# Moving a data-dependent branch behind a pair of expert products in a two-layer mixture-of-experts kernel

## The chip, the core and the metric

The kernel runs on one core of a Trainium2 chip, in one launch. The metric is the device time of that launch in microseconds. Before the change the median of three runs is 868.0 us (867.71 to 869.29); the execution that was profiled took 868.12 us.

The engines are called by their profile names: PE (matrix products; PEld is its weight load), DVE (the vector engine), ACT (the scalar engine), POOL (GpSimd), SP (the queue that issues the weight DMAs). Each engine runs its own list of instructions in order. A compiler step reorders the instructions of the kernel's text within the limits of their dependences and writes each engine's list down; a branch stands in the list of every engine that has an instruction in it.

## The reference, cut to what matters

Two transformer layers over 256 tokens of width 1024, in fp32. Each ends with a mixture of 16 experts, top 2 of one group of 4, which is what the change touches:

```python
def grouped_moe(h, router_w, router_bias, w_gate, w_up, w_down):
    ...
    combine = jnp.sum(jax.nn.one_hot(idx, N_EXPERTS, dtype=jnp.float32) * w[..., None], axis=1).astype(h.dtype)
    y = jnp.zeros_like(hf)
    for e in range(N_EXPERTS):
        a = jax.nn.silu(hf @ w_gate[e]) * (hf @ w_up[e])
        y = y + combine[:, e:e + 1] * (a @ w_down[e])
    return y.reshape(B, S, D)
```

Ahead of the experts of each layer stands an attention (forgetting attention in the first layer, latent attention in the second); between the layers the keys and values of the second are made.

## The kernel before, in words

`moe(l, ...)` is called once for each layer (l = 0, 1). A one-hot matrix `P` gathers up to `CAP = 64` tokens for each expert, so that the experts are worked in pairs, two of 64 rows, i = 0 to 7. For each pair the loop at the end of `moe` does:

- `wide("g", i, 4)`: the gate products, 16 matrix products into PSUM bank 4 (L899; each fp32 product shows as two records, so 32 records);
- ACT's silu of bank 4 (L984), while `wide("u", i, 5)` makes the up products in bank 5 (L899, 32 records);
- DVE's product of both (L995), the transposes (L1002), their copy `aT` (L1005, L1006);
- the down products in banks 6 and 7, in two halves p = 0, 1 (L1017, 16 records each), DVE's gate multiply `yb` (L1030) and the two parts `yh` (ACT L1032, DVE L1033);
- `scatter(i - 1)`: 8 products (L911) that add the pair before to the four accumulator banks 0 to 3. In the text it stands behind the up products of pair i.

After an odd pair, `fetch` gathers the tokens of the next four experts: products L869 into banks 5 and 4, copied out by ACT (L877) and DVE (L875); `slots(i + 1, 5)` makes the next pair's scatter matrix in bank 5 (L883, DVE L886 and L889).

Weights come in 1 MB units, four for the gate, four for the up and four for the down products of each pair, on SP's queue in the order of their use. `get` looks a unit up, `done` gives its place back, and only then SP issues a later unit (L250 into a ring, L262 into pieces of other tiles that have come free). They come to some 100 MB for a layer.

An expert may draw more than 64 tokens. `overflow()` covers that: each engine loads the largest count (L916) and takes the branch `tc.If(vmax > CAP)` (L917). Its body, which uses banks 5, 6 and 7, `yb`, the tiles of tag "t2" and the accumulators, is long and is not entered with these inputs: no instruction of it is in the trace. At the other end of the branch every engine raises its semaphores by what the body would have added, and goes on. An instruction behind the branch that shares a tile with the body waits for those raised counts; one that shares nothing doesn't. In the text the branch stands ahead of the gate products of pair `OV = 4`, the fifth. A hint to PE (`mark_branch_hint_location`, "LikelyTaken") names the target of the branch; it is queued behind the last down product of half p = 0 of the fourth pair.

Of the kernel before, what the change touches and what calls it, by code (L numbers as in the profile page):

```python
# [43 lines left out]
OV = 4  # L44
# [29 lines left out]
def trunk_kernel(ctx, tc, A, out):  # L74
# [10 lines left out]
    def bank(i):  # L85
        return psp.tile([128, 512], F32, name=f"b{i}", tag=f"b{i}")
# [11 lines left out]
    def wide_rows(nm, l, i):  # L98
        return ((0, 4), (4, 2), (6, 2)) if l and nm == "u" and i == E // 2 - 1 else ((0, 4), (4, 4))
# [165 lines left out]
    def give(l, *names):  # L265
        for tags in SPARE[l]:
            if tags[-1] in names:
                spare.append((l, tags))
        issue()

    def get(name):
        assert name in live, name
        return live[name]
# [11 lines left out]
    def done(name):  # L285
        assert stream[state["used"]][0] == name, (stream[state["used"]][0], name)
        drop()
        mods()
# [239 lines left out]
    def squares(t, half, junk=None, src=None):  # L528
        cs = slice(512 * half, 512 * half + 512)
        if junk is None:  # L530
            junk = big.tile([128, 512], F32, name="junk", tag="yb", bufs=2)
        SC.activation(junk, x[:, t, cs] if src is None else src, AF.Square, accum_out=ssq[:, t, half:half + 1])
# [214 lines left out]
    def moe(l, G, sh, acc):  # L747
# [112 lines left out]
        def fetch(g, c, b):  # L860

            if c % 2 == 0:
                XG[g, c // 2] = big.tile([128, 4, 256], F32, name="XG", tag="qa", bufs=2)
            dst = XG[g, c // 2]
            ps = bank(b)
            for kk in range(2):
                k = 2 * c + kk
                for n in range(4):
                    at = PE.matmul(ps[:, 256 * kk:256 * kk + 256], xs[n % 2, n // 2][:, 128 * k:128 * k + 128],  # L869
                                   P[g][:, n // 2].rearrange("p e s -> p (e s)"), start=n == 0, stop=n == 3)  # L870
            for kk in range(2):
                k = 2 * c + kk
                src = ps[:, 256 * kk:256 * kk + 256]
                if kk:
                    V.tensor_scalar(dst[:, k % 4, :], src, G[:, k:k + 1], sh[:, k:k + 1], op0=ALU.mult, op1=ALU.add)  # L875
                else:
                    SC.activation(dst[:, k % 4, :], src, AF.Identity, scale=G[:, k:k + 1], bias=sh[:, k:k + 1])  # L877
            return at.ins
# [12 lines left out]
        def wide(nm, i, b):  # L891
            ps = bank(b)
            for c, (k0, nk) in enumerate(wide_rows(nm, l, i)):
                ws = [get((nm, l, i, c, e)) for e in range(2)]
                for kk in range(nk):
                    k = k0 + kk
                    for e in range(2):
                        o = 128 * (i % 2) + 64 * e
                        last = PE.matmul(ps[64 * e:64 * e + 64, :], XG[i // 2, k // 4][:, k % 4, o:o + 64], ws[e][:, kk, :],  # L899
                                         start=k == 0, stop=k == 7).ins  # L900
                if i == 0 and nm == "g":
                    after[5] = last
                for e in range(2):
                    done((nm, l, i, c, e))
            return ps

        def scatter(i):
            for half in range(2):
                for t in range(T):
                    for j in range(2):  # L910
                        PE.matmul(acc[t, half], PT[i][:, t, :], yh[:, j, 512 * half:512 * half + 512],  # L911
                                  start=False, stop=False)
# [61 lines left out]
            SC.activation(bank_, x[:, t, 512 * half:512 * half + 512], AF.Copy)  # L974
        give(l, "x")
        for i in range(E // 2):
            if i == OV:
                overflow()
            pg = wide("g", i, 4)
            if l and i == 0 and G2IN:  # L980
                with behind(5):
                    fin_bc("g2_1", "g2")
# [10 lines left out]
            pu = wide("u", i, 5)  # L993
            a = wk.tile([128, F], F32, name="act", tag="t2", bufs=3)
            V.scalar_tensor_tensor(a, sg, cs[:, i:i + 1], pu, op0=ALU.mult, op1=ALU.mult)  # L995
            if i:
                scatter(i - 1)
            if l and i == 2:
                final_gain()
# [11 lines left out]
            for p, (c0, n) in enumerate(cols):  # L1011
                py = bank(6 + p % 2)
                cs_ = slice(c0, c0 + n)
                ws = [get(("d", l, i, p, e)) for e in range(2)]
                for k in range(4):
                    for e in range(2):
                        at = PE.matmul(py[64 * e:64 * e + 64, 0:n], aT[:, k, 64 * e:64 * e + 64], ws[e][:, k, :],  # L1017
                                       start=k == 0, stop=k == 3).ins
                if i == OV - 1 and p == 0:
                    with tc.issue_after(at):  # L1020
                        tc.mark_branch_hint_location(f"over{l}", "LikelyTaken", [mybir.EngineType.PE])
                for e in range(2):
                    done(("d", l, i, p, e))
                if p == 0 and turn_over:
                    for c in range(2, 4):
                        fetch(i // 2 + 1, c, (5, 4)[c % 2])
                if p == 0 and i < E // 2 - 1:
                    slots(i + 1, 5)
                yb = big.tile([128, 512], F32, name="yb", bufs=2)
                V.tensor_tensor(yb[:, 0:n], py[:, 0:n], M[f"g2_{l}"][:, cs_], op=ALU.mult)  # L1030
                if len(cols) == 2 or p == 0:
                    SC.activation(yh[:, 0, cs_], yb, AF.Copy)  # L1032
                    V.tensor_tensor(yh[:, 1, cs_], yb, yh[:, 0, cs_].bitcast(F32), op=ALU.subtract)  # L1033
                    parts_ = [(PT[i], yh[:, j, cs_]) for j in range(2)]
                else:
                    parts_ = [(PT[i].bitcast(F32), yb[:, 0:n])]
                if i == E // 2 - 1:
                    half, o = c0 // 512, c0 % 512
                    if l == 0 and p == 0:
                        x.new()  # L1040
                    for t in range(T):
                        for j, (pt, y_) in enumerate(parts_):
                            PE.matmul(acc[t, half][:, o:o + n], pt[:, t, :], y_, start=False,
                                      stop=o + n == 512 and j == len(parts_) - 1)
                        if o + n == 512:
                            ch = slice(512 * half, 512 * half + 512)
                            if l == 0:
                                V.tensor_copy(x[:, t, ch], acc[t, half])
                            squares(t, half, None, acc[t, half])
                    if l and o + n == 512:  # L1050
                        gains(half, acc)
# [337 lines left out]
```

## Time and profile before

| what | value |
|---|---|
| median of three runs | 868.0 us (867.71 to 869.29) |
| profiled execution | 868.12 us, of which the span from first to last instruction is 866.1 us |
| PE busy | 776.4 us, 90% of the span |
| DVE, ACT, POOL busy | 375.4, 266.3, 163.0 us |
| mean granted TensorE clock | 0.962 of full speed |
| read from HBM | 294.30 MB, 341 GB/s over the span |

The page of the profile gives busy times of the engines, the span in 40 slices (with the granted clock and the share of the DMA engines) and the costliest groups of instructions. The trace behind it tells each instruction's start, its time and, where an engine sat idle, what ended the wait. In a timeline a row is: start in us, duration in us, engine, line, operation, tiles, count of the merged instructions and, in brackets, the idle time ahead with the releaser. An engine name with a q (PEldq, DVEq) stands for its sequencer, which waits, branches and issues.

### The profile page before, as it was taken

The numbers are of one execution on the slowest core, as the hardware profiler recorded it, in microseconds if no ns is written. First come the engines' busy times: TensorE is split into PE (matmuls) and PEld (weight loads), VectorE is DVE, ScalarE is ACT, GpSimd is POOL, SyncE is SP. The second block draws the span as 40 slices with busy tenths as digits, with TensorE's granted clock in tenths as the row PEclk, the third lists the DMA queues.
The fourth block names the chain that finished last, engine by engine and source line by source line (L and its number), as shares of the span: only waits on it lengthen the run. The fifth ranks groups of instructions, "written<-read, shape, count | busy, mean of one in ns | idle before, by whom it ended". The sixth has DMA issues, their size and how long they took to land.

```text
span 866.1 us, 11932 instructions
## 1 busy us (share of the span) xinstructions
PE 776.4 (90%) x4522; PEld 447.1 (52%) x4522; DVE 375.4 (43%) x831; ACT 266.3 (31%) x578; POOL 163.0 (19%) x151
## 2 busy tenths in 40 slices
PE   5688999998999999999978998999799997999995
PEld 3477888665344343243336766876434343334332
DVE  2488599967122222131159867665412223022112
ACT  1346455543111010010045745866211111001002
POOL 1364477320000000000019653221000000000000
PEclk9599999999999999999989998999799999899998
DMA  9997797899999999999995969668599999999671
GB/s 346 384 375 278 264 347 278 306 390 392 418 394 393 415 409 402 410 414 405 404 403 184 303 222 406 230 231 297 186 398 391 416 403 398 400 401 391 260 274 66
DMA packets 102854, 296.31 MB, mean 342 GB/s; under 512 B 6992, under 2 KB 26624, under 8 KB 90496
## 3 DMA queue, kind: packets, MB, share of 16 engines
q1 hardware_dynamic: 101968, 293.79, 89.9%
q10 hardware_dynamic: 288, 1.05, 0.3%
q8 instruction: 38, 0.62, 0.3%
q0 software_dynamic: 528, 0.59, 0.2%
q14 instruction: 32, 0.26, 0.1%
HBM read 294.30 MB, written 1.05 MB: 341 GB/s over the span
## 4 chain that ended last, share of the span: by engine, by line
issue 29%; PE 24%; DVE 5%; DMA 2%; ACT 1%; POOLq 0%; POOL 0%; another core or an unknown queue 0%; ACTq 0%; DVEq 0%
PE b L899 7%; PE b L1017 4%; PE b L522 2%; PE b L523 2%; PE b L524 2%; DVE macc L329 1%; PE b L911 1%; DMA fg<-in_final_norm_g_dram 1%; DVE wl L518 1%; PE b L631 1%; DMA w<-in_w_mod_dram 1%; DMA w<-in_exp_w_gate_dram 1%; PE b L321 1%; PE b L593 1%; PE b L557 1%
## 5 line engine op out<-in xcount | busy, mean ns | idle before, releaser
L899 PE MATMUL b<-w,XG 128*64 128x512 f32 x1024 | 241.9, 596 | 6.5 <-DVEq L917 6.1
L518 POOL TENSOR_TENSOR wl<-w,wh 128x512 fp32r<-128x512 f32 (+3 forms) x90 | 129.3, 1450 | 357.0 <-ACT wh L517 349.7
L899 PEld LDWEIGHTS b<-w,XG 128*64 128x64 f32 x1024 | 77.5, 137 | 148.2 <-issue 142.1
L1017 PE MATMUL b<-w,aT 128*64 128x512 f32 (+1 forms) x528 | 125.6, 585 | 3.7 <-ACT aT L1005 3.7
L995 DVE SCALAR_TENSOR_TENSOR act<-sg,rcs,b 128x512 f32<-128x512 f32 x16 | 12.0, 747 | 222.9 <-PE b L899 222.9
L517 ACT ACTIVATE wh<-w 128x512 fp32r<-128x512 f32 (+3 forms) x136 | 76.6, 587 | 66.0 <-PE b L524 27.4
L1017 PEld LDWEIGHTS b<-w,aT 128*64 128x64 f32 x528 | 38.3, 136 | 66.4 <-issue 56.7
L329 DVE SCALAR_TENSOR_TENSOR macc<-w,cact,macc 128x1024 f32<-128x1024 f32 x42 | 63.7, 1517 | 2.5 <-DMA w<-in_w_mod_dram 2.0
L1032 ACT ACTIVATE yh<-yb 128x512 fp32r<-128x512 f32 x31 | 19.5, 630 | 116.6 <-DVE yb L1030 109.5
L518 DVE TENSOR_TENSOR wl<-w,wh 128x512 fp32r<-128x512 f32 (+2 forms) x46 | 44.2, 970 | 20.2 <-ACT wh L517 20.0
L1030 DVE TENSOR_TENSOR yb<-b,g 128x512 f32<-128x512 f32 (+1 forms) x33 | 22.2, 674 | 67.5 <-PE b L1017 67.5
L984 ACT ACTIVATE sg<-b 128x512 f32<-128x512 f32 x16 | 9.6, 597 | 134.1 <-PE b L899 134.1
L539 POOL TENSOR_TENSOR rs<-rs,mhalf 128x1 f32<-128x1 f32 (+1 forms) x9 | 5.4, 600 | 218.2 <-DVE rs L538 218.2
L524 PE MATMUL b<-h,wl 128*128 128x256 f32 (+1 forms) x136 | 41.1, 304 | 3.5 <-DVE wl L518 3.4
L522 PE MATMUL b<-h,wh 128*128 128x256 f32 (+1 forms) x136 | 41.0, 304 | 3.4 <-ACT h L579 3.4
L321 PE MATMUL b<-w,cact 128*32 128x256 f32 x512 | 39.8, 419 | 4.7 <-DMA w<-in_w_mod_dram 4.4
L869 PEld LDWEIGHTS b<-P,xs 128*128 128x128 f32 x256 | 34.4, 203 | 14.4 <-issue 6.9
L1005 ACT ACTIVATE aT<-b 128x256 f32<-128x256 f32 x16 | 6.1, 384 | 114.1 <-PE b L1002 114.1
L869 PE MATMUL b<-P,xs 128*128 128x256 f32 x256 | 39.1, 304 | 1.6 <-DVE P L834 1.6
L523 PE MATMUL b<-h,wh 128*128 128x256 f32 (+1 forms) x136 | 40.2, 296 | 0.0
L911 PE MATMUL b<-yh,PT 128*128 128x512 f32 x112 | 36.0, 438 | 2.7 <-ACT yh L1032 2.1
L911 PEld LDWEIGHTS b<-yh,PT 128*128 128x128 f32 x112 | 19.6, 197 | 28.2 <-issue 17.0
(296 smaller groups left out, 1230.0 us busy)
## 6 DMA issues: line engine op xcount, KB each, us to landing
w<-in_exp_w_down_dram SPq DMA_DIRECT2D x50, 1024.0 KB, 12.4
w<-in_w_mod_dram SPq DMA_DIRECT2D x48, 1024.0 KB, 9.0
w<-in_exp_w_gate_dram SPq DMA_DIRECT2D x48, 1024.0 KB, 12.4
w<-in_exp_w_up_dram SPq DMA_DIRECT2D x48, 1024.0 KB, 13.2
w<-in_a_w_in_dram SPq DMA_DIRECT2D x12, 1024.0 KB, 12.3
w<-in_exp_w_gate_dram SPq DMA_DIRECT2D x42, 256.0 KB, 7.1
w<-in_exp_w_up_dram SPq DMA_DIRECT2D x40, 256.0 KB, 6.6
w<-in_kv_w_mod_dram SPq DMA_DIRECT2D x8, 1024.0 KB, 7.4
```

Of the source, the lines that this page charges most:

```text
L321: PE.matmul(acc[32 * q:32 * q + 32, :], cact[:, k:k + 1].to_broadcast([128, 32]), w[:, kk, 256 * q:256 * q + 256], start=k == 0, stop=k == 7)
L329: V.scalar_tensor_tensor(acc, w[:, kk, :], cact[:, k:k + 1], acc, op0=ALU.mult, op1=ALU.add)
L517: SC.activation(hi, src, AF.Copy)
L518: lo_eng.tensor_tensor(lo, src, hi.bitcast(F32), op=ALU.subtract)
L522: PE.matmul(ps, l[0], r_[0], start=start, stop=False)
L523: PE.matmul(ps, l[0], r_[1], start=False, stop=False)
L524: PE.matmul(ps, l[1], r_[0], start=False, stop=stop)
L869: at = PE.matmul(ps[:, 256 * kk:256 * kk + 256], xs[n % 2, n // 2][:, 128 * k:128 * k + 128], P[g][:, n // 2].rearrange("p e s -> p (e s)" ...
L899: last = PE.matmul(ps[64 * e:64 * e + 64, :], XG[i // 2, k // 4][:, k % 4, o:o + 64], ws[e][:, kk, :], start=k == 0, stop=k == 7).ins
L911: PE.matmul(acc[t, half], PT[i][:, t, :], yh[:, j, 512 * half:512 * half + 512], start=False, stop=False)
L1017: at = PE.matmul(py[64 * e:64 * e + 64, 0:n], aT[:, k, 64 * e:64 * e + 64], ws[e][:, k, :], start=k == 0, stop=k == 3).ins
L1030: V.tensor_tensor(yb[:, 0:n], py[:, 0:n], M[f"g2_{l}"][:, cs_], op=ALU.mult)
```

## The change

In the text of the pair loop the gate products of every pair now stand first; at the fifth pair `scatter(3)` follows them, then the branch. `scatter` is left out at its old place for that pair. The hint for PE moves from half p = 0 to half p = 1 of the fourth pair's down products.

```diff
         for i in range(E // 2):
+            pg = wide("g", i, 4)
             if i == OV:
+                scatter(i - 1)
                 overflow()
-            pg = wide("g", i, 4)
...
-            if i:
+            if i and i != OV:
                 scatter(i - 1)
...
-                if i == OV - 1 and p == 0:
+                if i == OV - 1 and p == 1:
                     with tc.issue_after(at):
                         tc.mark_branch_hint_location(f"over{l}", "LikelyTaken", [mybir.EngineType.PE])
```

## Rows read from the trace of the kernel before

**Rows 1.** Page: busy us, share of the span, instructions.
```profile
PE 776.4 (90%) x4522; PEld 447.1 (52%) x4522; DVE 375.4 (43%) x831; ACT 266.3 (31%) x578; POOL 163.0 (19%) x151
```

**Rows 2.** PE's waits: waiter, releaser, total us, times, longest us.
```profile
PE b L899 <- DVEq L917: 6.1, 1, 6.1
```

**Rows 3.** Timeline of PE, second layer, about the branch.
```profile
728.38 1.22 PE L869 MATMUL b<-P,xs 128*128 128x256 f32 x8
729.44 0.35 PE L883 MATMUL b<-idc,P 128*128 128x160 f32 x2
730.09 0.46 PE L911 MATMUL b<-yh,PT 128*128 128x512 f32 x1 [0.30 <-PEq L917]
736.65 1.94 PE L899 MATMUL b<-w,XG 128*64 128x512 f32 x2 [6.10 <-DVEq L917]
738.52 3.35 PE L911 MATMUL b<-yh,PT 128*128 128x512 f32 x7
741.81 13.98 PE L899 MATMUL b<-w,XG 128*64 128x512 f32 x62
```

**Rows 4.** The branch's own line, second layer: durations in ns, first and last start.
```profile
L917 PEldq EVENT_SEMAPHORE  x2: 51/51/51, 729.8 to 730.0; - x2
...
L917 DVEq EVENT_SEMAPHORE  x2: 21/21/21, 736.5 to 736.6; - x2
L917 PEldq COMPARE_BRANCH  x1: 439/439/439, 728.6 to 728.6; - x1
...
L917 DVEq COMPARE_BRANCH  x1: 68/68/68, 730.8 to 730.8; - x1
L917 SPq COMPARE_BRANCH  x1: 53/53/53, 743.2 to 743.2; - x1
```

**Rows 5.** Timelines of DVE and of ACT, second layer, about the branch.
```profile
731.25 0.54 DVE L875 TENSOR_SCALAR XG<-b,c_sc,c_sh 128x256 f32<-128x256 f32 x1
...
752.45 0.60 ACT L984 ACTIVATE sg<-b 128x512 f32<-128x512 f32 x1 [22.05 <-PE b L899]
```

**Rows 6.** The branch's own line, first layer.
```profile
L917 DVEq EVENT_SEMAPHORE  x2: 21/21/21, 332.6 to 332.7; - x2
L917 PEldq COMPARE_BRANCH  x1: 482/482/482, 322.9 to 322.9; - x1
...
L917 DVEq COMPARE_BRANCH  x1: 72/72/72, 326.9 to 326.9; - x1
```

**Rows 7.** Timeline of PE, first layer, about the branch.
```profile
324.63 0.45 PE L883 MATMUL b<-idc,P 128*128 128x160 f32 x2
325.01 1.07 PE L899 MATMUL b<-w,XG 128*64 128x512 f32 x2
326.38 2.10 PE L911 MATMUL b<-yh,PT 128*128 128x512 f32 x8 [0.30 <-PEq L917]
328.42 13.95 PE L899 MATMUL b<-w,XG 128*64 128x512 f32 x62
```

**Rows 8.** Stretches: us, busy PE, PEld, DVE, ACT, POOL (count), granted clock, DMA share, GB/s.
```profile
735.10:741.90 6.80, 5.25 (x11) 2.54 (x13) 0.00 (x0) 0.00 (x0) 0.00 (x0) 0.50 1.05 385
...
801.00:866.00 65.00, 52.17 (x242) 19.97 (x240) 12.38 (x26) 7.77 (x17) 0.72 (x1) 0.96 0.55 201
```

**Rows 9.** Timeline of PE, second layer, the third pair, without a branch.
```profile
675.07 1.22 PE L869 MATMUL b<-P,xs 128*128 128x256 f32 x8
...
678.33 13.95 PE L899 MATMUL b<-w,XG 128*64 128x512 f32 x64
```

**Rows 10.** PE's waits, all of the stretch 742 to 866 us.
```profile
PE b L1002 <- DVE act L995: 3.7, 4, 0.9
PE b L1043 <- DVE yb L1030: 1.7, 1, 1.7
PE b L1017 <- ACT aT L1005: 1.2, 3, 0.5
```

**Rows 11.** The hint's instruction on PE's sequencer (it is on line 1385).
```profile
L1385 PEldq BRANCH_PREFETCH_HINT  x2: 41/43/45, 314.8 to 722.4; - x2
```

## The prediction

> **What bounds the kernel now.** I read the page first: PE is busy for 776.4 us of the 866.1 [rows 1], so the question is where PE stands still. The list of PE's waits names the branch: in one place PE waited 6.1 us for DVE at line 917 [rows 2]. The timeline of PE shows the place, the fifth pair of the second layer: after the slot products (L883) one scatter record at 730.09, then nothing until 736.65; two product records and seven scatter records then take 1.94 and 3.35 us, and only from 741.81 do the 62 others run at their usual pace [rows 3]. The branch's own line tells why: DVE branches at 730.8 and comes out on the other side, where it raises its semaphore, only at 736.5; PE had branched at 728.6 and was through at 729.8 [rows 4].
>
> Which product waited? The branch's body has DVE read bank 5, where the up products go, and not bank 4, where the gate products go. So an up product behind the branch waits for DVE's raised count and a gate product doesn't. In the second layer the compiler put up products first: ACT's silu, which needs the gate products, starts at 752.45 [rows 5], 3.3 us ahead of the end of all of them at 755.79. In the first layer DVE is away from 326.9 to 332.6 just as long [rows 6], but there PE was given gate products first, which run from 328.42, and only 0.30 us is lost [rows 7]. So it is one stall, in one layer, of an up product that stands too close behind DVE's branch.
>
> It costs more than 6.1 us. From 735.10 to 741.90 the granted clock is 0.50, the lower of the two levels (1.2 for 2.4 GHz), after that idle stretch; the 5.25 us of work in it [rows 8] would be 2.6 us at full clock.
>
> **The change, part by part.** *Gate products and scatter ahead of the branch.* Nothing is added or taken away: 16 gate products and 8 scatter products change places with the branch on PE. Then the up products come 7 us of gate products later, and DVE's absence lies beside these. Two measures of what PE would need there, both from the same work elsewhere:
> - The third pair of the second layer has the same products and no branch. From its last gather products at 675.07 to the end of its up products at 678.33 + 13.95 = 692.28 are 17.2 us [rows 9]. The fifth pair takes from 728.38 to 741.81 + 13.98 = 755.79, 27.4 us [rows 3]. Difference 10.2 us.
> - The fifth pair of the first layer, with the branch's short pause in it: from the slot products at 324.63 to 328.42 + 13.95 = 342.37, 17.7 us [rows 7]; in the second layer from 729.44 to 755.79, 26.35 us [rows 3]. Difference 8.6 us.
>
> The first has no pause at the branch, and a pause stays: PE finishes what it has, raises its counts and starts anew. Its price lies between the idle 0.30 us and what it does to the row: the two records at 325.01 are followed by the next at 326.38, 1.37 us later, where two take 13.95/32 = 0.44 [rows 7]: 0.93 us. So the gain is 10.2 - 0.93 = 9.3 by the one measure and 8.6 by the other; I take 8.9. As ends I keep 8.1 (8.6 less 0.5, the 17.2 and 17.7 of the two pairs differing by that much through the order of the products alone) and 9.9 (10.2 - 0.3).
>
> *Cover.* By the 17.7 us, of which the up products are the last 7.0, PE reaches them 10.7 us behind the slot products: at 740.2 in the second layer against DVE's 736.5, at 335.4 in the first against 332.6 [rows 4, 6]. The cover is 3.7 and 2.8 us. DVE has nothing else to do in the meantime: its last work ahead is L875 from 731.25 [rows 5], the next needs the up products. Should DVE branch later by more than the cover, each us more is lost on PE.
>
> *First layer.* There the pause only changes its place: 0, with -0.5 and +0.5 as ends, again by 17.2 against 17.7.
>
> *Other queues.* ACT's silu stays behind the branch. POOL is idle here (busy 0.00) [rows 8]. On SP the issue of the four units that follow the release of the gate's weights moves ahead of its branch, now at 743.2 [rows 4]. SP's branch takes 53 ns, and from 742 us to the end no wait of PE is for a weight [rows 10]: cost 0.
>
> *Does the gain live to the end?* From 742 us on PE waits only for DVE and ACT in its own chain, 3.7 + 1.7 + 1.2 = 6.6 us [rows 10]; from 801 us the DMA engines are busy 0.55 of the time [rows 8]. So the weights can come earlier as PE gives back places earlier, and the end moves with PE.
>
> *The hint.* It must leave PE time to have the code behind the branch. It ran at 722.4 and 314.8 [rows 11]; PE was through at 729.8 and 326.1 (the idle before 326.38) [rows 4, 7], so 7.4 us were enough. Behind half p = 1 it runs later, at most at 728.38, when those products are over [rows 3]; PE needs the code at 740.2. That leaves 11.8 us or more: cost 0. If it fails, see the second rival.
>
> Sum, on the profiled execution's own 868.1 us (span 866.1 and 2.0 around it; the median of the runs is 0.1 lower): 868.1 - 8.9 + 0 = 859.2 us, own range 857.7 (-9.9 - 0.5) to 860.5 (-8.1 + 0.5).
>
> **The rivals.**
> 1. *The branch stays where it was in PE's list.* The compiler orders by what is ready, and the branch is ready once the eight scatter products are issued; the gate products need bank 4, which DVE's L875 leaves at 731.25 + 0.54 = 731.8 [rows 5]. Against this: after the third pair's scatter the gate products came at once [rows 9], and in the text they now stand first. If it happens, up products wait for 736.5 as before; only the scatter (2.10 us in the first layer [rows 7]) fits into the wait. From 736.65, 64 records remain: at half clock some 12 of them until 741.9, the other 52 at 13.95/64 = 0.218 us, 11.3 us: end 753.2 for 755.8, gain 2.6, 865.5 us. With the full clock kept, 736.65 + 13.95 = 750.6, 862.9. With the hint too close (it needs up to 7.4 us, and may get 731.7 - 728.4 = 3.3) up to 4.1 us go in the first layer: 869.6.
> 2. *Slower: PE's code isn't there.* PE now passes 24 more products between hint and branch. If what the hint brought is not kept so long, PE pays what DVE pays without one: from its branch to 736.5 and 332.6, 5.6 us in both layers [rows 4, 6]. PE's sequencer runs ahead of its products by 0.8 us (729.0 to 729.8) [rows 4] to 2.7 us (323.4 to 326.1) [rows 6, 7]; idle remain 2.9 to 4.8 us, and the half clock behind, 2.6 more: about 6.5. In both layers: 859.2 + 13.0 = 872.2. In one layer alone 865.7. It decides from the point where both layers miss. For: DVE shows the price. Against: the hint has held over 7.4 and over 11.3 us already.
> The Trainium skill, page "Runtime: NRT & Kernel Launch", section "Instruction fetch mechanics", says that a taken branch to code outside an engine's current window must wait for a DMA to fetch it. DVE's rows fit this, SP's don't show it, and PE's are with a hint; by this rule alone, without the hint, PE would pay and the time would be this rival's 872.2.
> 3. *The lists change elsewhere.* All that follows is ordered anew with the branch. Pairs with equal work differ by 0.5 us; over the eight pairs from the fifth on in both layers that is 4 us at most: 855.2 to 863.2, and worse only if a wait is new.
>
> **How the numbers follow.** About 0.2% (1.7 us) is what a measurement of this kernel can tell from no change: below 866.3 is faster. Forecast 0.60. Rival 1: 0.14 (0.08 faster, 0.05 same, 0.01 slower). Rival 2: 0.10 in both layers (slower), 0.06 in one (0.03 faster, 0.03 same). Rival 3 beyond the forecast's range: 0.10 (0.05 faster, 0.03 same, 0.02 slower). Faster 0.76, same 0.11, slower 0.13. The range goes from 857.5 to 867.5 and leaves out rival 2 in both layers and the tails of 1 and 3, some 0.16.
>
> **What would show it.** Right: PE's wait at the branch falls from 6.1 us to a few tenths; no stretch of half clock near 735; the silu of the fifth pair of the second layer starts about 7 us ahead of the last up product; DVE's way through the branch still takes 5.6 us, unnoticed; from the slot products to the end of the up products 17.2 to 18.2 us in both layers. Wrong: an up product that still waits for DVE's line 917 (rival 1); a gap on PE behind its own branch of 3 to 5 us with nothing that released it (rival 2); waits for weights in the last pairs of the second layer, which would give part of the gain back.

## The result, and the profile after

The changed kernel takes 857.5 us, median of 4 runs (856.38 to 860.33); the kernel before takes 868.1 us beside it. The ratio is 0.988, with a 95% interval from 0.986 to 0.991. The median lies on the lower end of the stated range (857.5 to 867.5), 0.2 us below the own range of the sum (857.7 to 860.5). The profiled execution of the changed kernel took 856.4 us, with a span of 854.3 us. Lines behind the moved scatter are numbered one higher than before: L995 is L996, L984 is L985, L1017 is L1018.

The page, section 1, answers to [rows 1]:

```profile
PE 767.0 (90%) x4522; PEld 441.9 (52%) x4522; DVE 376.0 (44%) x831; ACT 266.6 (31%) x578; POOL 166.2 (19%) x151
```

PE does the same 4522 instructions in 9.4 us less of busy time. In the list of PE's waits the row of [rows 2] is gone; of line 917 only this one is left under L899 (total us, times, longest us):

```profile
PE b L899 <- PEq L917: 0.6, 2, 0.3
```

The timeline of PE in the second layer answers to [rows 3] (start us, us, line, operation, count, idle before and what ended it):

```profile
728.64 1.22 PE L869 MATMUL b<-P,xs 128*128 128x256 f32 x8
729.69 1.10 PE L911 MATMUL b<-yh,PT 128*128 128x512 f32 x4
730.63 0.35 PE L883 MATMUL b<-idc,P 128*128 128x160 f32 x2
730.82 1.15 PE L911 MATMUL b<-yh,PT 128*128 128x512 f32 x4
731.89 6.22 PE L899 MATMUL b<-w,XG 128*64 128x512 f32 x26
738.41 8.77 PE L899 MATMUL b<-w,XG 128*64 128x512 f32 x38 [0.30 <-PEq L917]
```

All eight scatter products and 13 of the 16 gate products (two records each) now stand ahead of the branch, which costs 0.30 us of idle time. ACT's timeline has the silu, which answers to [rows 5], 6.8 us ahead of the end of the up products at 738.41 + 8.77 = 747.18:

```profile
740.40 0.60 ACT L985 ACTIVATE sg<-b 128x512 f32<-128x512 f32 x1 [9.75 <-PE b L899]
```

The branch's own line there answers to [rows 4]:

```profile
L917 DVEq EVENT_SEMAPHORE  x2: 21/21/21, 737.2 to 737.3; - x2
L917 PEldq EVENT_SEMAPHORE  x2: 51/51/51, 738.2 to 738.3; - x2
...
L917 DVEq COMPARE_BRANCH  x1: 68/68/68, 731.4 to 731.4; - x1
L917 PEldq COMPARE_BRANCH  x1: 439/439/439, 733.3 to 733.3; - x1
```

DVE still needs 5.8 us from its branch at 731.4 to its raised count at 737.2; PE doesn't notice. And the stretch of [rows 8] is at full clock:

```profile
735.10:741.90 6.80, 6.50 (x31) 2.17 (x27) 0.00 (x0) 0.60 (x1) 0.00 (x0) 1.00 1.04 379
```

In the first layer it looks less well. The timeline of PE, which answers to [rows 7]:

```profile
320.92 1.07 PE L1018 MATMUL b<-w,aT 128*64 128x512 f32 x2
321.92 0.73 PE L911 MATMUL b<-yh,PT 128*128 128x512 f32 x2
322.58 3.65 PE L1018 MATMUL b<-w,aT 128*64 128x512 f32 x14
326.16 0.73 PE L911 MATMUL b<-yh,PT 128*128 128x512 f32 x2
326.73 0.35 PE L883 MATMUL b<-idc,P 128*128 128x160 f32 x2
327.01 1.07 PE L899 MATMUL b<-w,XG 128*64 128x512 f32 x2
328.01 0.73 PE L911 MATMUL b<-yh,PT 128*128 128x512 f32 x2
328.67 3.65 PE L899 MATMUL b<-w,XG 128*64 128x512 f32 x14
332.25 0.73 PE L911 MATMUL b<-yh,PT 128*128 128x512 f32 x2
333.28 10.52 PE L899 MATMUL b<-w,XG 128*64 128x512 f32 x48 [0.30 <-PEq L917]
```

The scatter, which stood in one piece in [rows 7], now comes in four pieces of two records, between down products (L1018) and gate products.

Where the time went is read best from the starts of DVE's act product (L995, now L996), one for each pair. Such an interval is the same to 0.05 us in all runs in which the order on PE is the same and no stretch of half clock falls into it. In the second layer the act products of the fourth and fifth pair start so, before and after:

```profile
715.47 0.75 DVE L995 SCALAR_TENSOR_TENSOR act<-sg,rcs,b 128x512 f32<-128x512 f32 x1 [10.49 <-PE b L899]
755.90 0.75 DVE L995 SCALAR_TENSOR_TENSOR act<-sg,rcs,b 128x512 f32<-128x512 f32 x1 [24.11 <-PE b L899]
```

```profile
715.73 0.75 DVE L996 SCALAR_TENSOR_TENSOR act<-sg,rcs,b 128x512 f32<-128x512 f32 x1 [10.48 <-PE b L899]
747.29 0.75 DVE L996 SCALAR_TENSOR_TENSOR act<-sg,rcs,b 128x512 f32<-128x512 f32 x1 [15.34 <-PE b L899]
```

So the interval of the fifth pair was 40.42 us (from the unrounded starts) and is 747.29 - 715.73 = 31.56: 8.86 less. The fifth pair of the first layer went from 31.69 to 33.25, 1.55 more. The sixth and seventh pairs of the second layer went from 28.30 to 27.15 and from 32.91 to 30.87, 3.19 less together. All other pairs, and the part behind the last act product (22.58 us), are as before. The stretch between the layers was 1.18 us shorter and the start 0.11; over all the runs below that stretch lies between 206.8 and 209.1 us and the start between 230.8 and 235.1, whatever the kernel, so this is chance. Sum: -8.86 + 1.55 - 3.19 = -10.5 from the change, and 1.3 from chance in this execution. 868.1 - 10.5 = 857.6, against the median of 857.5.

### The profile page after: what moved, and what is told of

The parts are those of the page before. It is cut to its first block, busy times and chain, and to the rows that moved or that the text cites. A ratio compares the mean times of both kernels' runs of the same rounds, so it can differ in the third digit from the quotient of the medians.

```text
span 854.3 us, 11932 instructions
## 1 busy us (share of the span) xinstructions
PE 767.0 (90%) x4522; PEld 441.9 (52%) x4522; DVE 376.0 (44%) x831; ACT 266.6 (31%) x578; POOL 166.2 (19%) x151
## 4 chain that ended last, share of the span: by engine, by line
issue 28%; PE 23%; DVE 5%; DMA 2%; ACT 1%; POOLq 0%; POOL 0%; SPq 0%; another core or an unknown queue 0%; DVEq 0%; ACTq 0%
PE b L899 6%; PE b L1018 4%; PE b L522 2%; PE b L523 2%; PE b L524 2%; DVE macc L329 1%; DMA fg<-in_final_norm_g_dram 1%; PE b L911 1%; PE b L631 1%; DMA w<-in_w_mod_dram 1%; DVE wl L518 1%; DMA w<-in_exp_w_gate_dram 1%; PE b L321 1%; PE b L557 1%; PE b L593 1%
## 5 line engine op out<-in xcount | busy, mean ns | idle before, releaser
L899 PE MATMUL b<-w,XG 128*64 128x512 f32 x1024 | 239.0, 595 | 0.6 <-PEq L917 0.6
L518 POOL TENSOR_TENSOR wl<-w,wh 128x512 fp32r<-128x512 f32 (+3 forms) x90 | 132.4, 1487 | 354.0 <-ACT wh L517 350.5
L899 PEld LDWEIGHTS b<-w,XG 128*64 128x64 f32 x1024 | 78.2, 137 | 140.8 <-issue 135.3
L1018 PE MATMUL b<-w,aT 128*64 128x512 f32 (+1 forms) x528 | 125.8, 585 | 3.7 <-ACT aT L1006 3.7
L996 DVE SCALAR_TENSOR_TENSOR act<-sg,rcs,b 128x512 f32<-128x512 f32 x16 | 12.0, 747 | 211.3 <-PE b L899 211.3
L1018 PEld LDWEIGHTS b<-w,aT 128*64 128x64 f32 x528 | 38.2, 136 | 66.0 <-issue 56.2
L985 ACT ACTIVATE sg<-b 128x512 f32<-128x512 f32 x16 | 9.6, 598 | 119.9 <-PE b L899 119.9
L523 PE MATMUL b<-wl,h 128*128 128x256 f32 (+1 forms) x96 | 30.0, 316 | 2.9 <-POOL wl L518 2.4
## 6 DMA issues: line engine op xcount, KB each, us to landing
w<-in_exp_w_gate_dram SPq DMA_DIRECT2D x48, 1024.0 KB, 12.8
```

The source lines that it names most:

```text
L518: lo_eng.tensor_tensor(lo, src, hi.bitcast(F32), op=ALU.subtract)
L523: PE.matmul(ps, l[0], r_[1], start=False, stop=False)
```

## The experiments

The medians, and the intervals that moved in more than one run, in us (from the profiled execution of each). The kernel before was run again beside each group of experiments, with medians from 867.9 to 869.2 us; the ratios below compare with these.

| kernel | median | first layer, pair 5 | pair 6 | second layer, pair 5 | pair 6 | pair 7 | pair 8 |
|---|---|---|---|---|---|---|---|
| before | 868.1 | 31.69 | 29.14 | 40.42 | 28.30 | 32.91 | 26.42 |
| after | 857.5 | 33.25 | 29.15 | 31.56 | 27.15 | 30.87 | 26.40 |
| e1 gate only | 869.0 | 31.68 | 29.14 | 40.43 | 28.30 | 32.89 | 26.41 |
| e2 scatter only | 857.3 | 33.25 | 29.14 | 31.56 | 27.15 | 30.87 | 26.40 |
| e3 second layer only | 856.6 | 31.68 | 29.14 | 31.57 | 27.15 | 30.87 | 26.41 |
| e4 short body | 862.4 | 31.67 | 29.16 | 34.86 | 28.30 | 32.88 | 26.41 |
| e5 no hint | 861.7 | 37.14 | 29.15 | 32.92 | 27.16 | 30.87 | 26.41 |
| e6 hint for DVE | 868.1 | 31.69 | 29.14 | 40.46 | 28.30 | 32.91 | 26.41 |
| e7 scatter held, one pair | 856.8 | 30.89 | 30.84 | 31.56 | 27.15 | 30.84 | 26.41 |
| e8 scatter held, all pairs | 858.6 | 30.87 | 26.26 | 32.29 | 27.14 | 30.52 | 25.24 |
| e9 DVE later | 863.7 | 34.63 | 30.84 | 34.72 | 27.15 | 30.87 | 26.41 |
| e10 second layer, held | 853.3 | 31.68 | 29.15 | 31.57 | 25.26 | 30.86 | 25.24 |
| e11 hint for DVE, near | 869.8 (one run) | 31.67 | 29.14 | 40.52 | 28.30 | 32.88 | 26.41 |
| e12 branch behind scatter | 854.7 | 31.68 | 29.15 | 31.58 | 25.26 | 30.85 | 25.23 |

In e8 others moved too: the third, fourth, seventh and eighth pair of the first layer (32.20, 25.30, 30.69 and 30.76, for 30.24, 26.45, 32.91 and 26.41) and the third and fourth of the second (29.16 and 26.95, for 30.24 and 23.06).

**Which of the two moves does it (e1, e2).** The kernel before with the gate products moved alone:

```diff
+            pg = wide("g", i, 4)
             if i == OV:
                 overflow()
-            pg = wide("g", i, 4)
```

> The kernel before with one line moved: the gate products stand ahead of the branch in the text; the fourth pair's scatter and the hint stay where they were. Theory (the scatter ahead of the branch is what moves the branch in PE's list: the branch's body writes the accumulators that the scatter writes, and has nothing to do with the gate's bank): PE's list and the time stay, 868.1 +- 1.0 us, with the wait of 6.1 us at DVE's L917 in the second layer. Rival (the gate products' place in the text does it): 857.5 us, and no such wait.

And with the scatter moved alone:

```diff
             if i == OV:
+                scatter(i - 1)
                 overflow()
             pg = wide("g", i, 4)
...
-            if i:
+            if i and i != OV:
                 scatter(i - 1)
```

> The kernel before with the fourth pair's scatter ahead of the branch; the gate products stay behind it in the text and the hint stays behind half p = 0. Theory (the scatter alone moves the branch; the gate products fill the time in which the accumulators are written): as after the change, 857.5 +- 1.5 us, the fifth pair of the second layer ends 31.6 us behind the fourth, and PE's wait at the branch is 0.3 us. Rival (both moves are needed): 868.1 us. If the hint's place counts as well, 1 to 5 us lie between this and 857.5.

With the gate alone the ratio to before is 1.001 (0.9999 to 1.0018), and the wait stands in the list of PE's waits:

```profile
PE b L899 <- DVEq L917: 6.1, 1, 6.1
```

With the scatter alone the ratio is 0.987 (0.985 to 0.989), and every interval is that of the changed kernel. So the scatter does it. The reason is read from the kernel's text: the branch's body adds into the same accumulators, so the branch must follow the scatter; the scatter waits for the fourth pair's last down products, and the compiler fills that time with gate products. Where the gate products stand in the text is of no account, nor is the hint's place: e2 has it behind half p = 0.

**What the first layer's 1.55 us are worth (e3).** The change in the second layer alone:

```diff
         for i in range(E // 2):
+            if l != 1 and i == OV:
+                overflow()
             pg = wide("g", i, 4)
-            if i == OV:
+            if l == 1 and i == OV:
                 scatter(i - 1)
                 overflow()
...
```

> The change in the second layer alone; in the first layer the text is that of before. Theory (the 1.55 us that the fifth pair of the first layer lost is the price of scatter products that stand singly between other products, and it is carried to the end): that pair's interval goes back to 31.7 us from 33.25, the fifth pair of the second layer keeps 31.6, and the time is 857.5 - 1.5 = 856.0 us. Rival (the 1.55 us is made up for later, by weights that come no earlier): 857.5 us with the interval at 31.7 all the same. Second rival (the interval differs by chance): 33.2 again.

The ratio is 0.9875 (0.9855 to 0.9895), the median 856.55 us. The interval is back at 31.68 and the second layer keeps its own. The medians of this and of the changed kernel are 0.9 us apart, less than the spread of either, so that the 1.55 us reach the end is read from the intervals: no later pair of the first layer is longer for it.

**What DVE's 5.6 us are (e4).** The kernel before with a branch body that covers the first expert only:

```diff
-                for e in range(E):
+                for e in range(1):
```

> The kernel before, with a branch body that covers the first expert alone instead of all of them (with these inputs the body is not run). Theory (DVE's 5.6 us at the branch is the time to get the code behind a long body): with the body so short DVE is through its branch in under 1 us, PE's wait of 6.1 us falls to under 1.5 us, the half clock from 735 us on is gone, and the time is 868.1 - (6.1 - 1.0) - 2.6 = 860.4 us, bounds 859 to 862. Rival (DVE's 5.6 us is a wait for something else, whatever the body's length): 868.1 +- 1.0 us with DVE's row as long as before.

The ratio is 0.994 (0.992 to 0.996). The branch's own line on DVE in the second layer:

```profile
L917 DVEq EVENT_SEMAPHORE  x2: 21/21/21, 733.9 to 734.0; - x2
L917 DVEq COMPARE_BRANCH  x1: 63/63/63, 732.9 to 732.9; - x1
```

And the stretch behind PE's wait, whose granted clock is the last column but two:

```profile
734.00:737.40 3.40, 3.36 (x6) 1.50 (x7) 0.00 (x0) 0.00 (x0) 0.00 (x0) 0.51 1.05 384
```

DVE is through in 1.0 us instead of 5.7 (in the first layer in 0.6 instead of 5.8), and PE's wait is 1.4 us. The DMA queues hint at what the difference is. In the kernel before, while DVE is away (730.85 to 736.5 us), these packets move beside the weights:

```profile
q8 instruction: 1, 0.02, 1.2%
q14 instruction: 2, 0.02, 0.9%
```

With the short body there is no instruction packet between 732.9 and 734.0. So a long body that is not run costs DVE 4.7 us more than a short one. That this is the fetch of the code behind it fits the packets, but no row ties a packet to an engine, and why ACT, which has no hint either, is through the branch in 0.4 us (730.3 to 730.7 after the change) is not shown. The time came out 0.4 us above the expected bounds because PE still got the lower clock for 3.4 us behind its 1.4 us of idle time (0.51 above), some 1.7 us that I had put at nothing.

**What the hint saves on PE (e5).** The changed kernel without it:

```diff
-                if i == OV - 1 and p == 1:
-                    with tc.issue_after(at):
-                        tc.mark_branch_hint_location(f"over{l}", "LikelyTaken", [mybir.EngineType.PE])
```

> The changed kernel without PE's hint. Theory (PE then pays at its branch what DVE pays, 5.6 us, less what PE's sequencer runs ahead of the products, 3.7 us in the first and 4.9 us in the second layer after the change): PE stands 1.9 us in the first layer and 0.7 us in the second, 857.5 + 2.6 = 860.1 us, and up to 863.5 if a stretch of half clock of 3.4 us (1.7 us each) follows. Rival (the full price of 5.6 us and the 2.6 us of half clock behind it in both layers, as rival 2 of the prediction has it without the run ahead): 870 us or more. Second rival (the hint does nothing): 857.5 us.

The ratio to before is 0.991 (0.988 to 0.994). PE's branch in the first and in the second layer:

```profile
L917 PEldq COMPARE_BRANCH  x1: 6088/6088/6088, 330.2 to 330.2; - x1
...
L917 PEldq COMPARE_BRANCH  x1: 6212/6212/6212, 738.5 to 738.5; - x1
```

And PE's wait behind it (total, times, longest):

```profile
PE b L899 <- PEq L917: 4.4, 2, 2.7
```

The branch alone takes 6.1 and 6.2 us, against 0.44 to 0.48 with the hint. Of that 2.7 and 1.7 us reach the products, because PE's sequencer runs ahead of them. The intervals grow by 3.89 us (2.4 more idle, and 1.5 from a stretch at the lower clock behind it) and by 1.36. So the theory's mechanism holds, though its waits were 0.8 and 1.0 us too short, and even without any hint the change would have been a gain. The profiled execution is the slowest of four (858.0 to 862.8 us); the median is 4.2 us above the changed kernel's.

**A hint for DVE (e6, e11).** The kernel before, with a second hint, first 15 us ahead of DVE's branch, then nearer:

```diff
...
+            if i == OV - 1:
+                with tc.issue_after(made):
+                    tc.mark_branch_hint_location(f"over{l}", "LikelyTaken", [mybir.EngineType.DVE])
```

> The kernel before with a hint for DVE's branch as well, behind the fourth pair's act product (L995), 15 us ahead of the branch; nothing is moved. Theory (DVE's 5.6 us at the branch is the time to get code that isn't there, and a hint brings it early): DVE is through in 0.5 to 1.1 us, PE's wait of 6.1 us falls to 0.3 to 1.4 us, and the time is 860 to 862.5 us, as with the short body (862.4). Rival (the hint doesn't help on DVE, or the code isn't kept for 15 us): 868.0 us.

> The kernel before with a hint for DVE's branch nearer to it, behind the subtraction at L1033 in the first half of the fourth pair's down products, some 3 us ahead of the branch in the second layer and 6 us in the first; the run with the hint 15 us ahead changed nothing. Theory (the hint was too early and what it brought was gone): in the first layer DVE is through its branch in about 1 us instead of 5.7, in the second in 2.5 us, and PE's wait there falls from 6.1 to 3 us: 862 to 865 us. Rival (a hint on DVE brings nothing here, whatever its lead): DVE takes 5.7 us in both layers, 868 us.

e6 is at 0.9996 (0.998 to 1.001). Its hint on DVE and DVE's branch:

```profile
L1388 DVEq BRANCH_PREFETCH_HINT  x2: 44/48/51, 313.0 to 716.6; - x2
...
L917 DVEq EVENT_SEMAPHORE  x2: 21/21/21, 737.6 to 737.7; - x2
L917 DVEq COMPARE_BRANCH  x1: 74/74/74, 731.9 to 731.9; - x1
```

The hint ran, and DVE needs 5.7 us all the same. From the hint to the branch there is one packet of q14, as many as without the hint, and two while DVE is away, as before. In e11 the hint ran at 728.6 us, 3.9 us ahead of the branch, and at 321.3, 6.3 us ahead: 5.7 and 5.8 us. The lead is not the difference to PE: in e2 PE's hint ran 14.6 and 10.6 us ahead of its branch (315.9 to 330.5 and 724.7 to 735.3 us), and the branch took 0.39 and 0.35 us. So what the hint does on PE it doesn't do on DVE here; why, stays open.

**What a scatter between products costs (e7, e8).** The changed kernel with the scatter ahead of the first layer's branch held behind the first half of the gate products, then with this for all pairs of both layers:

```diff
+                if nm == "g" and c == 0:
+                    first_half[i] = last
...
         def scatter(i):
-            for half in range(2):
+            with tc.issue_after(first_half[i + 1]) if l == 0 and i == OV - 1 else ExitStack():
+              for half in range(2):
```

> The changed kernel, with the eight scatter products ahead of the first layer's branch held together behind the first half of the gate products, instead of two and two between others. Theory (each place where 128-row scatter products stand between 64-column products costs some 0.4 to 0.6 us of PE beside their own time): the fifth pair's interval of the first layer falls from 33.25 to 31.5 us (31.3 to 31.9) and the time from 857.5 to 855.8 us. Rival (the 1.55 us is the branch's own price at its new place): the interval stays 33.2 and the time 857.5 us.

> As the last, but in all pairs of both layers the scatter stands in one piece behind the first half of the next pair's gate products. Theory (price by the place, as above): the fifth to eighth pairs of the first layer lose 1.6 + 3.2 + 1.4 + 0.5 us, the third 0.5, those of the second layer 2 in all: 857.5 - 9 = 848.5 us (846 to 852). Rival (weights and gathers come no earlier, so that PE waits for these instead): 855 to 858 us with new waits of PE for DMAs.

In e7 the fifth pair falls to 30.89, further than expected (31.3 to 31.9), but the time hardly moves (856.8 us, ratio 0.986, 0.982 to 0.989): in the profiled execution the next pair has 1.69 us more, with the same order on PE as before and a stretch at half clock from 358 to 362 us that before and after don't have. The four executions of e7 lie between 853.3 and 858.8 us, so how much of the shorter pair reaches the end is not shown. e8 is 858.6 us (0.989, 0.988 to 0.991), 0.6 above the rival's range and far from the theory's: the fourth to seventh pair of the first layer became shorter, and new waits of PE took part of it back.

```profile
PE b L899 <- DVE XG L875: 2.1, 1, 2.1
...
PE b L899 <- DMA w<-in_exp_w_up_dram: 1.9, 2, 1.4
...
PE b L899 <- DMA w<-in_exp_w_gate_dram: 1.3, 1, 1.3
...
PE b L1023 <- DMA w<-in_exp_w_down_dram: 0.5, 1, 0.5
```

Most of the waits for weights stand in the eighth pair of the first layer, which takes 30.76 us instead of 26.41. The seven intervals of the first layer sum to 199.9 us before, 201.4 after and 199.1 in e8, so with the scatter held everywhere the end of that layer waits for weights, and the layer is about a microsecond under its time before. In the second layer the rest is lost without a wait for a weight: the third and fourth pair take 56.1 us together instead of 53.3, the fifth 0.7 more (the wait for DVE's L875 in its gate products), and the last products ran at the lower clock in part, 1.0 us more.

**How much of DVE's absence is covered (e9).** The changed kernel with eleven more DVE operations ahead of the branch (its body reads their result, so that they stay ahead of it):

```diff
+            late_ = wk.tile([128, 256], F32, name="late_", bufs=1)
+            V.tensor_copy(late_, PT[OV].rearrange("p a b -> p (a b)").bitcast(F32))
+            for _ in range(10):
+                V.tensor_scalar(late_, late_, 1.0, 0.0, op0=ALU.mult, op1=ALU.add)
             vmax = nc.values_load(cmaxi[0:1, 0:1], min_val=0, max_val=S)
...
```

> The changed kernel with eleven more DVE operations on 128x256 tiles ahead of DVE's branch in both layers (they compute nothing that is used), so that DVE comes out of its branch later by d; from the rows of 128x256 operations d is 3 to 4.5 us. Theory (DVE's absence is covered by gate products alone, 1.9 us in the second layer from DVE's 737.2 to the first up product at 739.1, and 2.8 us in the first from 334.0 to 336.8): an up product waits for DVE's L917 again, d - 1.9 and d - 2.8 us; for d = 3.6 that is 1.7 + 0.8 us and 860.0 us (858.8 to 862, and up to 1.7 more for a stretch of half clock). Rival (nothing covers it): both layers pay all of d, 864.7 us. Second rival (no product waits for DVE any more): 857.5 us.

The ratio is 0.993 (0.991 to 0.995). PE in the second layer, and in the first:

```profile
735.79 7.09 PE L899 MATMUL b<-w,XG 128*64 128x512 f32 x32
745.45 7.07 PE L899 MATMUL b<-w,XG 128*64 128x512 f32 x24 [2.58 <-DVEq L921]
...
332.76 1.07 PE L899 MATMUL b<-w,XG 128*64 128x512 f32 x2
334.20 10.82 PE L899 MATMUL b<-w,XG 128*64 128x512 f32 x46 [0.36 <-PEq L921]
```

Counted from the slot products, DVE is out 4.2 us later than after the change in the second layer, and the first up product waits 2.58 us. Some 0.3 of that PE's own branch would have cost there anyway, so DVE's part is 2.3 and the cover 1.9 us, as the theory said. The compiler also moved PE's branch in that layer, from behind 13 gate products to behind all 16, so that no step of two products is broken there: 2.28 us more idle time and some 1.7 of half clock, less the 0.88 of the broken step (priced below), make the 3.16 us by which that interval grew. In the first layer DVE is 4.0 us later and PE loses some 0.3 us to it (10.82 for 46 records, against 10.52 for 48); the up products come later there too, since the compiler moved the branch by one product, of which more below. The theory holds. The time is above its range because d was 4.1 and not 3.6, half clock followed in the second layer, the move of the first layer's branch cost a microsecond, and the sixth pair of the first layer has the 1.69 us of e7 again (360 to 364 us at half clock).

**A version that beats both (e10, e12).** e3, with the scatter of the fifth to seventh pairs of the second layer held in one piece, and e12 with half of the fourth pair's as well:

```diff
...
-            for half in range(2):
+            with tc.issue_after(gate_at[i + 1]) if l and i >= OV else ExitStack():
+              for half in range(2):
```

> The change in the second layer alone, and there the scatter of the fifth to seventh pairs held in one piece behind gate products of the next pair (all of them for the fifth, the first half for the others). Theory (the later pairs of the second layer gained because scatter products stand in fewer places, and more of that is to be had): the intervals of the sixth to eighth pairs fall from 27.15, 30.87 and 26.40 to 25.3, 30.5 and 25.2 us, as in the run with the scatter held everywhere (30.52 and 25.24 there), and the time from 856.5 by 3.4 to 853 us. Rival (PE then waits for weights in the second layer as it did at the end of the first in that run): 855 to 856.5 us with waits of PE for DMAs at L899 or at the down products.

> As the run with the change in the second layer alone and the scatter held in one piece, with one more move: half of the fourth pair's scatter in the second layer stands behind the gate products, so that the branch follows scatter products instead of standing among gate products. Theory (the branch among products costs 1.3 us there, 31.57 against 30.24 for the same work without it, because they stop and start again; behind scatter products, where they stop anyway, it costs 0.2 to 0.3; the split scatter costs 0.4 more): the interval of the fifth pair of the second layer falls from 31.57 to 31.0 us (30.7 to 31.2), and the time from 853.3 by 0.6 to 852.7 us, which is within what the comparison can tell. Rival (the branch costs 1.3 us wherever it stands): the interval rises to 32.0 us.

e10 takes 853.3 us, 0.982 of before (0.981 to 0.983; the change alone is at 0.988). The sixth pair of the second layer:

```profile
759.00 7.04 PE L899 MATMUL b<-w,XG 128*64 128x512 f32 x32
765.96 2.13 PE L916 MATMUL b<-yh,PT 128*128 128x512 f32 x8
768.02 7.09 PE L899 MATMUL b<-w,XG 128*64 128x512 f32 x32
```

No wait for a weight is new in these pairs, and the sixth and eighth lose 1.9 and 1.2 us; the seventh, for which 30.5 was expected, loses nothing: half of its scatter stood beside the slot products after the change, and so made no place of its own. The profiled execution is the slowest of five (857.1 us): its start is 2.4 us longer than after the change, and its last products, at half clock from 844 us on, take 1.2 us more. e12 (854.7 us, 0.984, 0.981 to 0.986) is neither its theory nor its rival: the interval stays at 31.58. The gate products, which only half of the scatter now precedes, wait 0.45 us for DVE's L875, and PE stands 0.45 us behind the branch instead of 0.30; with the second piece of the scatter, some 0.36 us by the prices below, these take back the 0.88 that the branch's old place cost.

## Why the prediction was right, and where it was not

The stall and its price were right. That the time lies in the range is in part luck: the sum put the first layer and the later pairs at nothing, where they were +1.55 and -3.19 us, and the one took back half of the other.

**The stall (right).** An up product behind the branch waited for DVE, not for PE's own branch. e4 shortened DVE's absence and left PE's order as it was, and the wait went from 6.1 to 1.4 us; e9 lengthened it behind the change, and the wait came back.

**Its price, 8.9 us (right in size, 8.86).** The fifth pair of the second layer now has the same pieces in the same order as the third pair of both layers, which has no branch and takes 30.24 us. So before the branch cost 40.42 - 30.24 = 10.18 us, which is the prediction's 10.2 by the third pair. After it costs 31.56 - 30.24 = 1.32. The prediction's two terms for the remaining pause, 0.93 us by the row and the 8.6 of the other measure, lay on both sides of that, and the value between them met it. That it met it to 0.04 us is luck: the 0.93 holds the half step that is lost ahead of the branch and not the one behind it (0.44 each, below).

**The half clock (right).** No stretch of it is left near 735, as the row at 735.10 shows. It comes back where PE stands at the branch for longer: behind 1.4 us of idle time in e4, behind 2.7 in e5's first layer and behind 2.6 in e9, some 3.4 us of half clock each time (0.51, 0.56 and 0.59 over the stretch), though not behind 1.7 us in e5's second layer. The length of the pause does not decide it alone: in the sixth pair of the first layer PE stands 1.44 us for `yh` (ACT's L1032) with the same order in all these runs, and half clock followed in e7 and e9, not before or after the change.

**What moves the branch (right result, wrong reason).** Against rival 1 I argued that the gate products stand first in the text now. e1 shows that this does nothing. The scatter in front of the branch does it, and it takes 13 of the 16 gate products with it in the second layer and 8 in the first, not 16.

**Cover (too large).** I had 3.7 and 2.8 us. From the rows it is 2.1 us in the second layer and 2.8 in the first; e9 measured 1.9 in the second. (Three gate products are left behind the branch at 738.41 there; two run side by side, and the first up product beside the third, at 739.3, against DVE's 737.2.) The 17.7 us of the first layer were taken over to the second, where half of the scatter stands ahead of the slot products and the stretch is only 730.63 to 747.18, 16.6 us. In the first it is 17.1; both lie under the 17.2 to 18.2 that I named as the sign.

**The first layer, 0 with 0.5 either way (wrong, +1.55).** This is the term of the sum that failed. The pause only changed its place, as I said, but the scatter broke into four pieces, and I had no price for a place where scatter products stand among others. The rows have one. Records of gate, up and down products come two for each product, and the two experts' products of a step use 64 columns each. x2 takes 1.07 us and x4 1.08; x6 1.93 and x8 1.94; x10 and x12 both 2.79; x14 and x16 both 3.65. The sixth pair of the second layer shows it in two rows, after and before:

```profile
757.91 1.08 PE L899 MATMUL b<-w,XG 128*64 128x512 f32 x4
```

```profile
774.73 1.07 PE L899 MATMUL b<-w,XG 128*64 128x512 f32 x2
```

So a lone product takes as long as two that stand together, and what comes between the two products of a step wastes half a step, 0.44 us, on each side. A place between whole steps costs far less: 8 + 8 records take 1.87 + 1.87 from start to start in the seventh pair after, where 16 take 3.58, 0.16 more:

```profile
776.87 1.94 PE L1018 MATMUL b<-w,aT 128*64 128x512 f32 x8
778.74 1.21 PE L869 MATMUL b<-P,xs 128*128 128x256 f32 x8
...
789.94 3.65 PE L899 MATMUL b<-w,XG 128*64 128x512 f32 x16
793.52 1.20 PE L911 MATMUL b<-yh,PT 128*128 128x512 f32 x4
```

In the first layer's fifth pair there were two odd runs of products before (x2 and x62 in [rows 7]); there are four after (x2, x14, x2, x14): 0.88 us. And the scatter takes 0.66 us for two records from start to start, four times, in place of 2.04 for eight: 0.6. With 0.16 for the place ahead of the x48, between whole steps, that makes 1.6 for the 1.55 measured. e7 bears the price out: with the scatter in one piece between whole steps, four odd runs (1.76) and the 0.6 are gone, and the interval falls by 33.25 - 30.89 = 2.36.

The Trainium skill, page "TensorE: Matmul & The Clock Gate", section "Part 3: Packing small matmuls — row/col tiling", says that products which fill only a part of the array can be run side by side in it. The pairs of equal rows above agree; no row contradicts it.

**The later pairs (named, undersized).** Rival 3 said that the lists behind the branch are ordered anew, with up to 4 us either way. It was 3.19 us to the good, and by the same price. The sixth pair has two odd runs and four scatter places after, against four and five before (2 x 0.44, and 0.16 + 0.2 for a place and a piece of scatter: 1.24 for 1.15). In the seventh four odd runs fewer are 1.76 of its 2.04 us. e10, with no odd run and one place in the sixth pair, should be 0.88 + 3 x 0.36 = 1.96 below that; it is 1.89. These 3.19 us less the first layer's 1.55 are the 1.6 by which the time lies under 859.2.

**The branch's own 1.32 us.** In the second layer the branch stands between products 13 and 14: an odd run on both sides, 0.88 us, beside 0.30 us of idle time and 0.16 for the place. In the first layer it stands where the scatter has broken the products already; there the seventh pair has the same pieces in the same order, without a branch, and takes 32.91 to the fifth's 33.25: 0.34. e9 moved that branch by one product, into a step, and the interval grew by 1.38, of which 0.3 is the wait for DVE.

**Rival 2 (did not happen, and its price was too high).** The hint ran 7.6 and 7.4 us ahead of PE's branch (725.65 to 733.25, 321.94 to 329.29), much as before (6.2 and 8.1 to the branch itself); my 11.8 counted to the products that need the code, which is 12.8 in the second layer (to 738.41). PE was through in time, and so it was with 14.6 us in e2. Without it (e5) the loss is 5.25 us in the two layers of the profiled execution together, not 13: the branch takes 6.1 to 6.2 us, somewhat more than DVE's 5.5 to 5.8, but PE runs further ahead at the new place than at the old, and half clock followed in one layer only. The Trainium skill, page "Runtime: NRT & Kernel Launch", section "Instruction fetch mechanics", has the rule that a taken branch to code outside the engine's window waits for a DMA; e4, where neither the wait nor an instruction packet is there, and e5 agree with it.

**Other queues, and the end (right).** No row of SP, ACT or POOL is new among PE's waits, and the 22.58 us behind the last act product are unchanged. That weights come early enough, which I read for the second layer alone, holds in the first only just, as e8 shows.

## What to carry to other kernels

A branch around a long body can stop an engine for microseconds although the body isn't entered (4.7 us more than around a short one, on DVE); put work between it and the first instruction that needs the other engine's raised count. What moved the branch here was work that its body depends on (the scatter into the accumulators that the body writes), not the place of independent work in the text. When products run in twos side by side, let nothing come between the two, and look at the counts of the rows: odd runs are lost half steps.

## What was unexpected

- A lone product of 64 columns costs as much as the two of a step (1.07 for x2, 1.08 for x4), so a scatter or a branch inside a step costs 0.88 us more than one between steps, which costs 0.16.
- The hint worked on PE (0.44 us against 6.1 at its branch) with leads of 6.2 to 14.6 us, and did nothing on DVE with leads of 15, 6.3 and 3.9 us (5.5 to 5.8 us each).
- Without the hint a branch of PE takes 6.1 to 6.2 us, and 1.7 to 2.7 of it reach the products.
